# Two-layer hybrid encoder: the loaded up-projection weights begin 64 bytes behind a multiple of 256

## Chip, cores and metric

The kernel runs on 1 core of one Trainium2 chip, in one launch. The metric is the device time of the whole program in microseconds (us), lower is better; the time before is the median of 3 runs. TensorE (PE) does the matmuls and has its own weight-load queue (PEld), VectorE (DVE) and ScalarE (ACT) do the elementwise work, GpSimd (POOL) a little of it, and SyncE (SP) issues the transfers.

## Reference, cut to what matters

Two layers over 256 tokens of width 2048, all in float32. Each layer is a mixer (windowed attention beside a bidirectional mLSTM) between two large projections, and an MLP with a squared ReLU:

```
h   = rms_norm(x, g_pre_mix)
mix = concat(attention, mlstm)(h @ w_in) @ w_out      # w_in 2048x4624, w_out 2048x2048
x   = x + rms_norm(mix, g_post_mix)
h   = rms_norm(x, g_pre_mlp)
u   = square(relu(h @ w_up))                          # w_up 2048x8192
x   = x + rms_norm(u @ w_down, g_post_mlp)            # w_down 8192x2048
```

## The kernel before

**Three products for one.** Each float32 matrix is split into two parts of type float32r, `hi` (a rounded copy) and `lo` (the rest). A product is made of three matmuls: hi times hi, hi times lo, lo times hi. For weights, `load` does the split: SyncE fetches a piece of 1 MB into `raw` (2 buffers), ACT copies it to `whi` (line 188), DVE subtracts to get `wlo` (line 189). `whi` and `wlo` have 4 buffers each in pool `wsp`. Tokens are split in the same way and stand transposed in tiles of pool `tpool` (`hT`, `attT`, `memT`, `h2T`, `uT`), 16 KB per partition, the two parts of a block of 128 features side by side.

**Two forms of a stage.** A stage is a matrix block of 2048 x 512 (four pieces). In the streaming form (`mm_tile`, `mm_k`, lines 200 to 202) TensorE loads a 128 x 128 block of the tokens and streams 512 columns of the weights past it; the result has tokens on the partitions. All of w_in, w_out, w_down and the first up stage of each layer are done so. In the stationary form (`mm_stationary`, lines 269 to 271) it loads a 128 x 128 block of the weights and streams all 256 tokens past it, so that the result comes out transposed, as the down projection wants it. The other 15 up stages of each layer are done so: 15 stages x 64 blocks x 3 = 2880 matmuls a layer, 5760 in all. `stationary(key)` says which form a stage has. Each matmul, in both forms, has a weight load of its own.

**Addresses.** A partition's tiles follow each other in the order of the pools. The small tiles of pool `edge` come first and end at byte 2048. In the program before, every T tile, every `whi`, `wlo` and `raw` buffer begins at a multiple of 256 bytes, and within a stationary piece the blocks are 512 bytes apart, within a T tile 512 or 1024. One input stage (number 3: the gates with a part of q and k) is 272 columns wide, so that its blocks, 1088 bytes apart, begin 0, 64, 128 and 192 bytes behind a multiple of 256 in turn.

**Order.** The stages run in the order of `STAGES`. `mm_tile` and `mm_stationary` call `load` for their own stage and the one after, and `pump` puts steps of the mixer's side work between the matmuls of the input stages. The side work's temporaries of 1 KB (`rbt`, `cy`, `cth`, `kw`, `qw`, `ht`) share pool `f1k`.

Of the kernel before, what the change touches and what calls it, by code (L numbers as in the profile page):

```python
# [11 lines left out]
F32R = mybir.dt.float32r  # L12
# [5 lines left out]
P = 128  # L18
# [57 lines left out]
def stationary(key):  # L76


    _, st, b, n = key
    return st == "up" and (b, n) != (0, 0)  # L80
# [6 lines left out]
def encoder_kernel(ctx, tc, x, wall, rope, conv_w, gate_bias, ml_g, sink, gpre, gpost, out):  # L87
# [3 lines left out]
    wsp = ctx.enter_context(tc.tile_pool(name="wsp", bufs=4))  # L91
# [2 lines left out]
    apool = ctx.enter_context(tc.tile_pool(name="apool", bufs=1))  # L94
    gpool = ctx.enter_context(tc.tile_pool(name="gpool", bufs=3))
    f2k = ctx.enter_context(tc.tile_pool(name="f2k", bufs=8))
    f1k = ctx.enter_context(tc.tile_pool(name="f1k", bufs=5))
    small = ctx.enter_context(tc.tile_pool(name="small", bufs=3))
    lay = ctx.enter_context(tc.tile_pool(name="lay", bufs=2))
    psmm = ctx.enter_context(tc.tile_pool(name="psmm", bufs=2, space=bass.MemoryType.PSUM))  # L100
# [57 lines left out]
    order = []  # L158
# [9 lines left out]
    def load(i, begin=None):  # L168


        if i >= len(order) or order[i] in pieces:
            return
        o, w = offs[order[i]]
        k, n = (KC, P) if stationary(order[i]) else (PK, w)
        got = []
        for q in range(NPC):
            raw = wraw.tile([P, k, n], F32, tag="raw", name="raw")
            a = o + q * P * k * n
            src = wall[a:a + P * k * n].rearrange("(p k n) -> p k n", p=P, k=k)
            if begin is not None:  # L180
                begin(q)
            hi = wsp.tile([P, k, n], F32R, tag="hi", name="whi")
            lo = wsp.tile([P, k, n], F32R, tag="lo", name="wlo")
            step = 1 if begin is not None and q < 2 else k
            for j in range(0, k, step):
                sl = slice(j, j + step)
                nc.sync.dma_start(raw[:, sl], src[:, sl])
                nc.scalar.activation(hi[:, sl], raw[:, sl], AF.Copy)  # L188
                nc.vector.tensor_tensor(out=lo[:, sl], in0=raw[:, sl], in1=hi[:, sl].bitcast(F32), op=ALU.subtract)  # L189
            got.append((hi, lo))  # L190
        pieces[order[i]] = got
# [25 lines left out]
    def mm_tile(key, T, stages=(), after=None, at=None, half=False):  # L217

        load(pos[key])
        load(pos[key] + 1)
        if stages:
            ps = [psmm.tile([P, NT, 512], F32, tag="mm", name="mm")[:, 0] for _ in range(NT)]
# [30 lines left out]
    def mm_stationary(key, T, after):  # L256

        load(pos[key])  # L260
        load(pos[key] + 1)
        both = psmm.tile([P, 2, 512], F32, tag="mm", name="mms")
        for pair in range(2):
            ps = both[:, pair].rearrange("p (i t) -> p i t", i=2)
            for i in range(2):
                hi, lo = pieces[key][2 * pair + i]
                for k in range(KC):
                    Tk = T[k // 8][:, k % 8]
                    nc.tensor.matmul(ps[:, i], lhsT=hi[:, k], rhs=Tk[:, 0], start=(k == 0), stop=False)  # L269
                    nc.tensor.matmul(ps[:, i], lhsT=hi[:, k], rhs=Tk[:, 1], start=False, stop=False)  # L270
                    nc.tensor.matmul(ps[:, i], lhsT=lo[:, k], rhs=Tk[:, 0], start=False, stop=(k == KC - 1))  # L271
            after(pair, ps)
# [369 lines left out]
    def begin(q):  # L642
        if q:
            load_x(1, q - 1)
            load_x(0, q)
# [310 lines left out]
```

## Time and profile before

| | us |
|---|---|
| median of 3 runs | 2176.94 |
| the runs | 2176.94, 7516.22, 2171.56 |
| the profiled execution | 2173.81 |
| its span, first to last instruction | 2172.0 |
| PE busy, PEld busy | 2130.1, 1884.1 |
| DVE busy, ACT busy | 1136.4, 983.3 |

The profiled execution lies 0.14% under the median; 1.8 us of it lie outside the span. The records of matmuls overlap (a record of a 256-column float32r matmul lasts 0.28 us while one starts every 0.12 us), so a matmul's price is the distance from its start to the next one's start, and not its record's length.

### The profile page before, as it was taken

The numbers are of one execution on the slowest core, as the hardware profiler recorded it, in microseconds if no ns is written. First come the engines' busy times: TensorE is split into PE (matmuls) and PEld (weight loads), VectorE is DVE, ScalarE is ACT, GpSimd is POOL, SyncE is SP. The second block draws the span as 40 slices with busy tenths as digits, with TensorE's granted clock in tenths as the row PEclk, the third lists the DMA queues.
The fourth block names the chain that finished last, engine by engine and source line by source line (L and its number), as shares of the span: only waits on it lengthen the run. The fifth ranks groups of instructions, "written<-read, shape, count | busy, mean of one in ns | idle before, by whom it ended". The sixth has DMA issues, their size and how long they took to land.

```text
span 2172.0 us, 28977 instructions
## 1 busy us (share of the span) xinstructions
PE 2130.1 (98%) x12412; PEld 1884.1 (87%) x12412; DVE 1136.4 (52%) x1219; ACT 983.3 (45%) x1077; POOL 60.7 (3%) x68
## 2 busy tenths in 40 slices
PE   8999999999999999999999999999999999999998
PEld 6878887988998998898878788879889989989986
DVE  6666566444445444445576656464444444444454
ACT  6445445443443443344354555354444434433542
POOL 0000003000000000000020000030000000000000
PEclk9999999999999999999999999999999999999999
DMA  7534354555545555546544344545554555554553
GB/s 254 175 133 162 136 202 146 194 197 194 190 177 194 177 189 196 193 157 210 175 177 168 126 146 156 201 157 178 210 194 176 187 192 181 179 194 174 185 207 116
DMA packets 62209, 388.37 MB, mean 179 GB/s; under 512 B 9600, under 2 KB 10112, under 8 KB 17280
## 3 DMA queue, kind: packets, MB, share of 16 engines
q1 hardware_dynamic: 61936, 386.48, 50.8%
q8 instruction: 97, 1.59, 0.3%
q14 instruction: 32, 0.26, 0.0%
q10 hardware_dynamic: 144, 0.03, 0.0%
HBM read 384.39 MB, written 2.10 MB: 178 GB/s over the span
## 4 chain that ended last, share of the span: by engine, by line
PE 93%; DVE 2%; ACT 2%; DMA 1%; POOL 1%; issue 1%; SPq 0%; POOLq 0%; DVEq 0%; ACTq 0%
PE mm L202 19%; PE mm L201 19%; PE mm L200 19%; PE mms L269 11%; PE mms L271 11%; PE mms L270 11%; DMA raw<-wall 1%; PE pn L591 1%; PE sc L375 1%; DVE xs L789 1%; PE po L414 1%; DVE wlo L189 1%; POOL h2T L322 0%; ACT uz L845 0%; ACT whi L188 0%
## 5 line engine op out<-in xcount | busy, mean ns | idle before, releaser
L189 DVE TENSOR_TENSOR wlo<-raw,whi 128x2048 fp32r<-128x2048 f32 (+3 forms) x374 | 828.7, 2217 | 907.2 <-ACT whi L188 906.7
L188 ACT ACTIVATE whi<-raw 128x2048 fp32r<-128x2048 f32 (+3 forms) x374 | 692.9, 1853 | 943.9 <-PE mm L202 514.6
L269 PE MATMUL mms<-h2T,whi 128*128 128x256 f32 x1920 | 544.4, 284 | 7.3 <-ACT uz L845 7.3
L270 PE MATMUL mms<-h2T,whi 128*128 128x256 f32 x1920 | 542.6, 283 | 0.0
L271 PE MATMUL mms<-h2T,wlo 128*128 128x256 f32 x1920 | 539.8, 283 | 0.0
L201 PE MATMUL mm<-wlo,uT 128*128 128x512 f32 x1024 | 398.4, 389 | 0.0
L200 PE MATMUL mm<-whi,uT 128*128 128x512 f32 x1024 | 398.4, 389 | 0.0
L202 PE MATMUL mm<-whi,uT 128*128 128x512 f32 x1024 | 398.1, 389 | 0.0
L269 PEld LDWEIGHTS mms<-h2T,whi 128*128 128x128 f32 x1920 | 368.4, 192 | 11.9 <-ACT uz L845 11.5
L270 PEld LDWEIGHTS mms<-h2T,whi 128*128 128x128 f32 x1920 | 368.4, 192 | 0.3
L271 PEld LDWEIGHTS mms<-h2T,wlo 128*128 128x128 f32 x1920 | 366.9, 192 | 0.0
L200 PE MATMUL mm<-whi,hT 128*128 128x512 f32 (+2 forms) x640 | 242.6, 380 | 8.7 <-ACT hT L321 6.5
L202 PE MATMUL mm<-whi,hT 128*128 128x512 f32 (+2 forms) x640 | 242.0, 379 | 0.3 <-POOL hT L322 0.2
L201 PE MATMUL mm<-wlo,hT 128*128 128x512 f32 (+2 forms) x640 | 241.3, 377 | 0.2 <-DVE wlo L189 0.2
L201 PEld LDWEIGHTS mm<-wlo,uT 128*128 128x128 f32 x1024 | 192.2, 188 | 40.0
L200 PEld LDWEIGHTS mm<-whi,uT 128*128 128x128 f32 x1024 | 192.2, 188 | 39.5
L202 PEld LDWEIGHTS mm<-whi,uT 128*128 128x128 f32 x1024 | 192.2, 188 | 39.4
L200 PEld LDWEIGHTS mm<-whi,hT 128*128 128x128 f32 x640 | 121.9, 190 | 29.1 <-ACT hT L321 7.4
L202 PEld LDWEIGHTS mm<-whi,hT 128*128 128x128 f32 x640 | 121.7, 190 | 21.9 <-POOL hT L322 1.2
L201 PEld LDWEIGHTS mm<-wlo,hT 128*128 128x128 f32 x640 | 121.9, 191 | 20.4 <-DVE wlo L189 0.5
L866 DVE SCALAR_TENSOR_TENSOR A_mlp<-mm,s2q,A_mlp 128x512 f32<-128x512 f32 x48 | 34.0, 747 | 37.0 <-PE mm L202 37.0
L200 PE MATMUL mm<-whi,memT 128*128 128x512 f32 x128 | 50.4, 394 | 0.0
(221 smaller groups left out, 1463.8 us busy)
## 6 DMA issues: line engine op xcount, KB each, us to landing
raw<-wall SPq DMA_DIRECT2D x350, 1024.0 KB, 4.8
raw<-wall SPq DMA_DIRECT2D x8, 544.0 KB, 3.6
g<-gpost SPq DMA_DIRECT2D x16, 256.0 KB, 4.5
raw<-wall SPq DMA_DIRECT2D x8, 512.0 KB, 3.3
xs<-x_in SPq DMA_DIRECT2D x8, 256.0 KB, 5.2
raw<-wall SPq DMA_DIRECT2D x8, 256.0 KB, 6.6
y_out<-xs SPq DMA_DIRECT2D x8, 256.0 KB, 2.8
cossin<-rope SPq DMA_DIRECT2D x1, 256.0 KB, 7.0
```

The lines of the kernel that those rows point to most:

```text
L188: nc.scalar.activation(hi[:, sl], raw[:, sl], AF.Copy)
L189: nc.vector.tensor_tensor(out=lo[:, sl], in0=raw[:, sl], in1=hi[:, sl].bitcast(F32), op=ALU.subtract)
L200: nc.tensor.matmul(dst, lhsT=xh, rhs=hi, start=(k == 0), stop=False)
L201: nc.tensor.matmul(dst, lhsT=xh, rhs=lo, start=False, stop=False)
L202: nc.tensor.matmul(dst, lhsT=xl, rhs=hi, start=False, stop=(k == KC - 1))
L269: nc.tensor.matmul(ps[:, i], lhsT=hi[:, k], rhs=Tk[:, 0], start=(k == 0), stop=False)
L270: nc.tensor.matmul(ps[:, i], lhsT=hi[:, k], rhs=Tk[:, 1], start=False, stop=False)
L271: nc.tensor.matmul(ps[:, i], lhsT=lo[:, k], rhs=Tk[:, 0], start=False, stop=(k == KC - 1))
L375: nc.tensor.matmul(sc[:, j], lhsT=qT[:, q0 + j, t * P:(t + 1) * P], rhs=kT[:, g], start=(j == 0), stop=False)
L414: nc.tensor.matmul(po[:, j], lhsT=vA[:, kb, g * HD:(g + 1) * HD], rhs=pT[:, kb], start=(kb == 0), stop=(kb == 1))
L591: nc.tensor.matmul(pn[:, :DV + 1], lhsT=dt[:, d, c], rhs=va[:, c, h], start=True, stop=(c == c1))
L866: nc.vector.scalar_tensor_tensor(out=acc[:, t, sl], in0=ps, scalar=s2[t], in1=acc[:, t, sl], op0=ALU.mult, op1=ALU.add)
```

## The change

The `whi` and `wlo` buffers get 64 elements (256 bytes) more. A stage of the stationary form uses its buffer from element 16 on, which is 64 bytes behind the buffer's start; a stage of the streaming form uses it from element 0. A buffer is 2112 x 4 = 8448 bytes, 33 times 256, so all buffers still begin at a multiple of 256. Eight buffers take 2048 bytes more; pool `f1k` gives up one of its five buffers (1024 bytes). No instruction is added or removed, and all shapes stay.

```diff
-    f1k = ctx.enter_context(tc.tile_pool(name="f1k", bufs=5))
+    f1k = ctx.enter_context(tc.tile_pool(name="f1k", bufs=4))
...
-            hi = wsp.tile([P, k, n], F32R, tag="hi", name="whi")
-            lo = wsp.tile([P, k, n], F32R, tag="lo", name="wlo")
+
+            o1 = 16 if stationary(order[i]) else 0
+            hi, lo = (
+                wsp.tile([P, 2048 + 64], F32R, tag=x, name=f"w{x}")[:, o1:o1 + k * n].rearrange(
+                    "p (k n) -> p k n", k=k) for x in ("hi", "lo"))
```

## Rows read from the trace of the kernel before

**Rows 1.** The page's busy time by engine, and TensorE's granted clock in 40 slices.
```profile
PE 2130.1 (98%) x12412; PEld 1884.1 (87%) x12412; DVE 1136.4 (52%) x1219; ACT 983.3 (45%) x1077; POOL 60.7 (3%) x68
...
PEclk9999999999999999999999999999999999999999
```
**Rows 2.** The page's chain that ended last, by engine and by line.
```profile
PE 93%; DVE 2%; ACT 2%; DMA 1%; POOL 1%; issue 1%; SPq 0%; POOLq 0%; DVEq 0%; ACTq 0%
PE mm L202 19%; PE mm L201 19%; PE mm L200 19%; PE mms L269 11%; PE mms L271 11%; PE mms L270 11%; DMA raw<-wall 1%; PE pn L591 1%; PE sc L375 1%; DVE xs L789 1%; PE po L414 1%; DVE wlo L189 1%; POOL h2T L322 0%; ACT uz L845 0%; ACT whi L188 0%
```
**Rows 3.** Windows (PE, PEld, DVE, ACT, POOL, clock, DMA, GB/s): stationary, then streaming.
```profile
600.00:620.00 20.00, 20.00 (x169) 20.00 (x168) 6.32 (x4) 8.61 (x8) 0.00 (x0) 1.00 0.44 159
700.00:720.00 20.00, 20.00 (x90) 16.55 (x89) 8.84 (x6) 7.67 (x4) 0.00 (x0) 1.00 0.58 200
```
**Rows 4.** Waits, 390 to 1080 us: total us, times, longest us.
```profile
ACT whi L188 <- PE mms L270: 159.1, 40, 7.0
ACT whi L188 <- DMA raw<-wall: 16.2, 18, 4.5
```
**Rows 5.** Groups by line: count, busy us, mean ns, idle before and its end.
```profile
L269 PE MATMUL mms<-h2T,whi 128*128 128x256 f32 x1920 | 544.4, 284 | 7.3 <-ACT uz L845 7.3
```
**Rows 6.** Timeline of TensorE in a stationary stage: first and last of 16 matmuls (start, duration).
```profile
596.68 0.28 PE L271 MATMUL mms<-h2T,wlo 128*128 128x256 f32 x1
...
598.48 0.28 PE L271 MATMUL mms<-h2T,wlo 128*128 128x256 f32 x1
```
**Rows 7.** Timeline of TensorE in a down stage: first and last of 18 matmuls.
```profile
699.62 0.39 PE L200 MATMUL mm<-whi,uT 128*128 128x512 f32 x1
...
703.47 0.39 PE L202 MATMUL mm<-whi,uT 128*128 128x512 f32 x1
```
**Rows 8.** Timeline: plain float32 matmuls (four in a row), then streams behind them.
```profile
74.99 1.02 PE L375 MATMUL sc<-scr 128*128 128x256 f32 x4
...
75.97 0.40 PE L202 MATMUL mm<-whi,hT 128*128 128x512 f32 x1
76.20 0.40 PE L200 MATMUL mm<-whi,hT 128*128 128x512 f32 x1
76.44 0.39 PE L201 MATMUL mm<-wlo,hT 128*128 128x512 f32 x1
...
77.13 0.39 PE L201 MATMUL mm<-wlo,hT 128*128 128x512 f32 x1
```
**Rows 9.** Line 375 alone: duration in ns, least, median and most.
```profile
L375 PE MATMUL sc<-scr x64: 377/379/635, 75.0 to 1212.7; 128*128 128x256 f32 x64
```
**Rows 10.** Timeline of the 272-column stage: first of each six matmuls, four blocks.
```profile
98.36 0.28 PE L200 MATMUL mm<-whi,hT 128*128 128x272 f32 x1
...
99.11 0.28 PE L200 MATMUL mm<-whi,hT 128*128 128x272 f32 x1
...
99.86 0.29 PE L200 MATMUL mm<-whi,hT 128*128 128x272 f32 x1
...
100.62 0.28 PE L200 MATMUL mm<-whi,hT 128*128 128x272 f32 x1
...
101.36 0.39 PE L200 MATMUL mm<-whi,hT 128*128 128x512 f32 x1
```
**Rows 11.** Weight loads by line: stationary stages, then down stages.
```profile
L270 PEld LDWEIGHTS mms<-h2T,whi 128*128 128x128 f32 x1920 | 368.4, 192 | 0.3
...
L200 PEld LDWEIGHTS mm<-whi,uT 128*128 128x128 f32 x1024 | 192.2, 188 | 39.5
```
**Rows 12.** Timeline of VectorE around the fullest moment of pool `f1k`.
```profile
64.42 0.87 DVE L357 SCALAR_TENSOR_TENSOR rbt<-mm,r_s,cossin 128x256 f32<-128x256 f32 x2
...
65.86 0.86 DVE L357 SCALAR_TENSOR_TENSOR rbt<-mm,r_s,cossin 128x256 f32<-128x256 f32 x2
66.64 0.75 DVE L360 TENSOR_TENSOR ra<-ra,rbt 128x256 f32<-128x256 f32 x2
...
69.51 0.75 DVE L360 TENSOR_TENSOR ra<-ra,rbt 128x256 f32<-128x256 f32 x2
```

## Prediction

> **What bounds the kernel now.** I read the page's busy times first, then the chain, then windows by stage, then single starts on the timeline. TensorE is busy 98% of the span at the granted clock of the upper level (2.4 GHz) in every slice [rows 1], and 93% of the chain is TensorE's own work: 57% in the streaming lines 200 to 202, 32% in the stationary lines 269 to 271 [rows 2]. In a stationary stretch and in a streaming one there is no idle time on it at all, while VectorE and ScalarE work less than half of the time [rows 3]. The weights are no bound there: the split's first step waits for TensorE to give its buffers back, 159.1 us in 40 waits on the stationary line alone, and for the transfer only 16.2 us in 18 [rows 4]. TensorE waits for the stationary results' evacuation 7.3 us in all [rows 5]. So the time is the number of matmuls times the distance of their starts, and the change can act on that distance alone.
>
> **What a matmul costs.** Sixteen stationary matmuls start at 596.68 to 598.48 us: 1.80 us over 15 steps, 120.0 ns each [rows 6]. The 256 columns take 256/2.4 = 106.7 ns, so 13.3 ns are extra. In the down stage 17 steps take 3.85 us, 226.5 ns each for 512 columns (213.3 ns): the same 13 ns [rows 7]. The extra belongs to the matmul, or to its load, and not to the columns. Plain float32 matmuls have nearly none of it: four of them last 1.02 us from first start to last end [rows 8], each lasts 379 ns [rows 9], so the starts are (1020 - 379)/3 = 214 ns apart, for 256 columns at half rate (213.3 ns); the printed hundredths leave this open by some 3 ns, and I take 2 ns of extra. They too have a load each. What costs 11 ns arises, then, where a load and a stream at full rate read together. All of them begin at multiples of 256 bytes now. That is what the change alters, for 3 x 1920 = 5760 matmuls [rows 5]; 1 ns on each is 5.76 us, 0.26% of the time.
>
> **The change part by part.** *The 64 bytes.* No row of before shows a load that begins 64 bytes behind its stream. Bound from below: the 2 ns of the plain float32 rows instead of 13.3 ns, 11 ns x 5760 = 63 us less [rows 8, 9]. Bound from above: behind a disturbance, with the same addresses, streams start up to 0.24 us apart (76.20 to 76.44) and five steps take 1.16 us, 232 ns each, before they settle to 226.7 [rows 8]; the largest is some 9 ns over the settled distance, and 9 x 5760 = 52 us more. That the distance moves at all with equal addresses says that the extra is no fixed price but hangs on how load and stream fall together in time.
> The nearest row is the 272-column stage. There the loaded tokens begin at a multiple of 256 and the streamed weights 0, 64, 128 and 192 bytes behind one, block after block. The six matmuls of a block take 0.75, 0.75, 0.76 and 0.74 us [rows 10], which is 125.0, 125.0, 126.7 and 123.3 ns each, for 272/2.4 = 113.3 ns of columns: an extra of 11.7, 11.7, 13.3 and 10.0 ns. The fourth is the one in which the load stands 64 bytes past the stream modulo 256, as after the change. If a shift by 64 bytes freed the readers of each other, one of the four would have shown 115 ns. None did. The difference between the fourth and the first is 1.7 ns, printed to within 3 ns, and between the fourth and the settled 13.3 ns it is 3.3 ns. I take 1.5 ns less, 1.5 x 5760 = 8.6 us, with 3 ns less and 2 ns more as its own bounds (-17 to +12 us). Against that row speaks that its offset lasts six matmuls only, in which a pattern that needs several to settle (rows 8) may not have come about; so both far ends stay open.
> The Trainium skill speaks against any effect: "SBUF — State Buffer", section "Who interferes with whom", gives TensorE two independent read ports, one for the streamed operand and one for the load, and says that it never waits on anyone. By that the sum would be nothing for this part; the 13 ns that float32r streams pay and plain float32 ones don't, and the unsettled 232 ns, fit it badly.
> *A shorter stationary stage.* At the lower bound a stage of 192 matmuls takes 20.9 us in place of 23.0, still not under the 96 x 226.5 ns = 21.7 us of a streaming one by much, whose weights come in time at 200 GB/s [rows 3]. The waits of the split are for TensorE, so a gain in it would not be taken back by the transfers.
> *The load's own length* is recorded as 192 ns in the stationary stages and 188 in the down stages [rows 11]; a change of these 4 ns goes along with the distance and is not counted again.
> *One temporary less in `f1k`.* The fullest moment that I find has four buffers in use: two pairs of `rbt` are written at 64.42 and 65.86 us and read at 66.64 and 69.51 us [rows 12]. The fullest moment elsewhere is no fuller, worked out from first write and last read of each user. So four suffice and the sum has +1 us for it; should VectorE wait at the four such places as long as its step between the two reads (2.9 us less 0.75 us), it is 9 us. Its cover is that TensorE has the input stages' matmuls to go on with.
> *Copies and subtractions* into a buffer that begins 64 bytes on: same shapes, and both engines have room [rows 3]; nothing.
>
> **The sum.** The profiled execution took 2173.8 us, its span 2172.0 and 1.8 outside; the median of the runs is 3.1 us above it, and I start between them, at 2175. 2175 - 9 + 1 = 2167 us.
>
> **The rivals.** *The address is of no account* (what costs is the load itself, at any address). For it: the four offsets of rows 10 give nearly the same. Then 2175 + 1 = 2176 us.
> *Load and stream stop colliding.* For it: the plain float32 rows show that a load need not cost more than 2 ns, and the extra is equal in both forms. Against it: rows 10. Between 109 and 112 ns in place of 120: 46 to 63 us less, 2112 to 2129 us. The Trainium skill's "TensorE: Matmul & The Clock Gate", section "Back-to-back issue gap", has N/2.4 + 2.5 ns for a warm matmul alone, which is 109.2 ns here; the trace's 120 is over it, and the gap between them is 62 us, about this rival's most.
> *The shifted load falls into a worse pattern and stays there*, the other side: what rows 8 show for some matmuls becomes the settled state of the stationary stages. Unsettled steps average 232 against 226.7, 5 ns; 4.5 ns x 5760 = 26 us, 2201 us. It is slower as soon as the distance settles above 120 ns, and by over 2% (43.5 us) from 127.6 ns on, near the largest single step seen.
> *Only the lost temporary is felt*: 2175 + 9 = 2184 us.
>
> **How the numbers follow.** Forecast (a small gain, 2159 to 2188 as its own range) 0.38; no account 0.22; no collision 0.24; worse pattern 0.11; temporary 0.05. The likeliest is 2167 us. The range must take in the collision rival, with which, the address rival and the temporary it holds 0.89: from 2112, less 2 for the runs' scatter, to 2190, 2110 to 2190 us. About 2% is what a measurement of this kernel can tell from no change. Faster by over 2% (under 2133 us) is the collision rival but for a part of it, 0.22; slower by over 2% (above 2220 us) is the end of the worse pattern, 0.05; within 2%, 0.73.
>
> **What would show it.** Starts on the timeline of a stationary stage after the change: 117 to 122 ns apart is the forecast or the address rival (exactly 120.0 is the latter), 109 to 112 the collision rival, 124 and more the worse pattern. The down stages should stay at 226.5 ns, TensorE's share of the busy time and the clock should stay, and ScalarE's wait for line 270 should be there still; if a gain on the distance doesn't reach the time, its idle time before line 269 will have grown. The temporary's cost would show as VectorE's waits before `rbt` and `cth` and as TensorE's idle time before 280 us and between 1105 and 1360 us. I am wrong if the settled distance in the stationary stages isn't what the short runs of rows 10 let expect: a pattern that settles over hundreds of equal matmuls can end elsewhere.

## The result, and the profile after

The changed kernel took 2144.73 us (median of 4 runs, 2141.79 to 2146.77) against 2174.25 us before (median of 4 runs: 2168.82, 2171.56, 2176.94 and 7516.22). The run of 7516.22 us counts in that median, as in the 2176.94 us of the prediction; without it the median before is 2171.56 us. The ratio leaves it out: 0.987, 95% interval 0.984 to 0.990. The profiled execution has a span of 2143.4 us, 28.6 us under that of before. All lines behind the diff have moved by three: 200 to 202 are 203 to 205, 269 to 271 are 272 to 274.

The page of the changed kernel, busy time by engine, then the chain by engine and by line; it answers to [rows 1, 2]:

```profile
PE 2100.0 (98%) x12412; PEld 1855.3 (87%) x12412; DVE 1135.4 (53%) x1219; ACT 983.9 (46%) x1077; POOL 60.8 (3%) x68
...
PE 92%; DVE 2%; DMA 2%; ACT 2%; POOL 1%; issue 1%; SPq 1%; POOLq 0%; DVEq 0%; ACTq 0%
PE mm L205 19%; PE mm L204 19%; PE mm L203 19%; PE mms L272 10%; PE mms L274 10%; PE mms L273 10%; DMA raw<-wall 1%; PE sc L378 1%; PE pn L594 1%; DVE xs L792 1%; PE po L417 1%; DVE wlo L192 1%; POOL h2T L325 1%; ACT whi L191 0%; ACT uz L848 0%
```

The reader is to see that counts and DVE and ACT stay, that TensorE's busy time falls by 30.1 us, about what the span lost, and that of TensorE's lines in the chain the stationary ones alone lose a share. TensorE is as much the bound as before.

The groups by line of the changed kernel, which answer to [rows 5, 11]:

```profile
L272 PE MATMUL mms<-h2T,whi 128*128 128x256 f32 x1920 | 535.2, 279 | 7.0 <-ACT uz L848 6.8
...
L273 PEld LDWEIGHTS mms<-h2T,whi 128*128 128x128 f32 x1920 | 362.3, 189 | 0.3
```

The waits of the changed kernel from 390 to 1080 us, which answer to [rows 4]:

```profile
ACT whi L191 <- PE mms L273: 126.6, 33, 6.8
ACT whi L191 <- DMA raw<-wall: 35.7, 25, 3.6
```

TensorE's idle time before a stationary line is 7.0 us (7.3 before). The recorded load is 3 ns shorter, and that of the down stages stays at 188. The split still waits for TensorE first of all; its wait for transfers is up from 16.2 us, but TensorE didn't wait for it, so the weights are no bound.

The timeline of TensorE in the changed kernel, which answers to [rows 6, 7]: first and last of 21 matmuls of a stationary stage, a wait in it, first and last of 22 matmuls behind that wait, and first and last of 17 matmuls of a down stage:

```profile
559.81 0.28 PE L274 MATMUL mms<-h2T,wlo 128*128 128x256 f32 x1
...
562.16 0.28 PE L273 MATMUL mms<-h2T,whi 128*128 128x256 f32 x1
...
573.47 0.28 PE L272 MATMUL mms<-h2T,whi 128*128 128x256 f32 x1
573.59 0.28 PE L273 MATMUL mms<-h2T,whi 128*128 128x256 f32 x1
574.32 0.39 PE L272 MATMUL mms<-h2T,whi 128*128 128x256 f32 x1 [0.45 <-ACT uz L848]
574.54 0.28 PE L273 MATMUL mms<-h2T,whi 128*128 128x256 f32 x1
574.66 0.28 PE L274 MATMUL mms<-h2T,wlo 128*128 128x256 f32 x1
...
575.25 0.28 PE L273 MATMUL mms<-h2T,whi 128*128 128x256 f32 x1
575.36 0.28 PE L274 MATMUL mms<-h2T,wlo 128*128 128x256 f32 x1
...
589.75 0.28 PE L274 MATMUL mms<-h2T,wlo 128*128 128x256 f32 x1
...
592.13 0.28 PE L274 MATMUL mms<-h2T,wlo 128*128 128x256 f32 x1
...
699.66 0.39 PE L204 MATMUL mm<-wlo,uT 128*128 128x512 f32 x1
...
703.28 0.39 PE L205 MATMUL mm<-whi,uT 128*128 128x512 f32 x1
```

2.35/20 is 117.5 ns, 2.38/21 is 113.3 ns, 3.62/16 is 226 ns. There are two distances where there was one: group by group of 48 matmuls (one weight buffer) the stationary stages start 117.8 ns or 113.3 ns apart, in nearly all groups from first to last (120.0 before), and the streaming stages haven't moved. Between the two places lies the wait at 573 us. TensorE stands still there for 0.45 us, until ScalarE has taken the results out; some seven matmuls follow at 0.12 us, and then it goes on at 0.11 (113.3) for stages. Instructions and addresses modulo 256 are the same on both sides of that wait. The buffers themselves, 33 times 256 bytes apart, begin at even and odd multiples of 256 in turn, and the groups from all of them start alike: no period longer than 256 bytes shows.

From the starts on the timeline I sum two times for each kernel. S is the time of all stretches of stationary matmuls, each from its first start to the next streaming matmul's start; T is the rest of the span from the first streaming start on. Before: S 698.4, T 1465.0 us. After: S 670.8, T 1464.2 us. So 27.6 of the span's 28.6 us were won in the stationary stages, 27.6/5760 = 4.8 ns on each matmul.

### The profile page after: what moved, and what is told of

Its sections match the earlier page's. It is cut to its first block, busy times and chain, and to the rows that moved or that the text cites. A ratio compares the mean times of both kernels' runs of the same rounds, so it can differ in the third digit from the quotient of the medians.

```text
span 2143.4 us, 28980 instructions
## 1 busy us (share of the span) xinstructions
PE 2100.0 (98%) x12412; PEld 1855.3 (87%) x12412; DVE 1135.4 (53%) x1219; ACT 983.9 (46%) x1077; POOL 60.8 (3%) x68
## 4 chain that ended last, share of the span: by engine, by line
PE 92%; DVE 2%; DMA 2%; ACT 2%; POOL 1%; issue 1%; SPq 1%; POOLq 0%; DVEq 0%; ACTq 0%
PE mm L205 19%; PE mm L204 19%; PE mm L203 19%; PE mms L272 10%; PE mms L274 10%; PE mms L273 10%; DMA raw<-wall 1%; PE sc L378 1%; PE pn L594 1%; DVE xs L792 1%; PE po L417 1%; DVE wlo L192 1%; POOL h2T L325 1%; ACT whi L191 0%; ACT uz L848 0%
## 5 line engine op out<-in xcount | busy, mean ns | idle before, releaser
L272 PE MATMUL mms<-h2T,whi 128*128 128x256 f32 x1920 | 535.2, 279 | 7.0 <-ACT uz L848 6.8
L273 PE MATMUL mms<-h2T,whi 128*128 128x256 f32 x1920 | 533.3, 278 | 0.0
L274 PE MATMUL mms<-h2T,wlo 128*128 128x256 f32 x1920 | 530.5, 278 | 0.0
L272 PEld LDWEIGHTS mms<-h2T,whi 128*128 128x128 f32 x1920 | 360.7, 188 | 11.8 <-ACT uz L848 11.1
L273 PEld LDWEIGHTS mms<-h2T,whi 128*128 128x128 f32 x1920 | 362.3, 189 | 0.3
L274 PEld LDWEIGHTS mms<-h2T,wlo 128*128 128x128 f32 x1920 | 360.0, 188 | 0.0
```

## The experiments

Three theories stood. *Distance*: what counts is how far the loaded block stands from the streamed one, modulo some multiple of 64 bytes. *Own start*: a load that begins at 64 modulo 256 is cheaper by itself. *By-product*: the moved buffers or the smaller `f1k` pool change the order or the waits. All edits below are to the changed kernel; the distance is load minus stream, modulo 256 bytes.

| kernel | stationary distance | streaming distance | time, us | S, us | T, us | stationary starts, ns | 512-column starts, ns |
|---|---|---|---|---|---|---|---|
| before | 0 | 0 | 2174.25 | 698.4 | 1465.0 | 120.0 | 226.7 |
| changed | 64 | 0 | 2144.73 | 670.8 | 1464.2 | 113.3 or 117.8 | 226.7 |
| e1 | 0 | 0 | 2175.21 | 698.5 | 1466.7 | 120.0 | 226.7 |
| e4 (all moved) | 0 | 0 | 2172.66 | 698.5 | 1464.2 | 120.0 | 226.7 |
| e7 | 32 | 0 | 2166.05 | 689.1 | 1466.6 | 118.3 | 226.7 |
| e8 | 96 | 0 | 2156.58 | 684.0 | 1462.7 | 117.3 or 118.6 | 226.7 |
| e2 | 128 | 0 | 2169.51 | 693.6 | 1465.9 | 118.6 or 120.0 | 226.7 |
| e3 | 192 | 0 | 2155.05 | 680.5 | 1465.1 | 113.3 or 117.8 | 226.7 |
| e6 | 64 | 192 | 2149.64 | 664.9 | 1477.5 | 113.3 or 117.8 | 229 |
| e5 | 64 | 64 | 2170.01 | 663.6 | 1496.0 | 113.3 or 117.8 | 233.3 |
| e10 | 64 | 128 | 2175.51 | 674.6 | 1491.0 | 113.3 or 117.8 | 232.4 |
| e9 | 64 | 0, last piece 64 | 2142.09 | 665.4 | 1464.9 | 113.3 or 117.8 | 226.7 |
| e11 | 64 | 0, 272 columns 64 | 2148.31 | 674.2 | 1464.0 | 113.3 or 117.8 | 226.7 |
| e12 | 64 | 0 | 2146.97 | 671.9 | 1465.9 | 113.3 or 117.8 | 226.7 |

The times of e5, e6, e9 and e12 are medians of several runs, those of e1 to e4, e7, e8, e10 and e11 single ones; the runs of the kernel before beside them have medians of 2171 to 2173 us. The starts are medians of the settled groups (for 512 columns in e5, e6 and e10 the mean, since they settle less).

**e1, the room alone.**

```diff
-            o1 = 16 if stationary(order[i]) else 0
+            o1 = 0 if stationary(order[i]) else 0
```

> The wider buffers and the f1k pool of four, but every stage from element 0 on. If the 64 bytes are the cause of the 30 us, stationary starts are 120.0 ns apart again and the time is that of before, 2168 to 2177 us. If the moved buffers or the smaller pool (through another order on the engines) are the cause, starts stay between 113 and 118 ns apart and the time near 2145 us.

2175.21 us beside 2172.82 before. First and last of 22 stationary matmuls of e1 on the timeline:

```profile
599.83 0.28 PE L273 MATMUL mms<-h2T,whi 128*128 128x256 f32 x1
...
602.35 0.28 PE L273 MATMUL mms<-h2T,whi 128*128 128x256 f32 x1
```

2.52/21 = 120.0 ns. The by-product theory falls: S is that of before to 0.1 us, T 1.7 us more, which is within what T differs by between runs (1463 to 1467 us in kernels that share it).

**e4, everything moved by 64 bytes.**

```diff
-    nhalf = edge.tile([P, 16], F32, name="nhalf")
+    nhalf = edge.tile([P, 32], F32, name="nhalf")
...
-            o1 = 16 if stationary(order[i]) else 0
+            o1 = 0 if stationary(order[i]) else 0
```

> A small tile ahead of the pools grows by 64 bytes, so tokens, streamed and loaded weights all begin 64 bytes behind a multiple of 256; no stage has an offset of its own. Relative-offset theory: the distance is nothing again, 120 ns in the stationary and 226.7 in the streaming stages, about 2172 us. Own-start theory (a load that begins at 64 modulo 256 is cheaper by itself): stationary 113 to 118 ns, about 2145 us, and the streaming stages, whose loaded tokens then begin at 64 too, nearer 222 ns, about 2115 us in all.

2172.66 us. First and last of 22 stationary matmuls, then of 17 in a down stage of e4:

```profile
599.77 0.28 PE L273 MATMUL mms<-h2T,whi 128*128 128x256 f32 x1
...
602.29 0.28 PE L273 MATMUL mms<-h2T,whi 128*128 128x256 f32 x1
...
699.65 0.39 PE L205 MATMUL mm<-whi,uT 128*128 128x512 f32 x1
...
703.27 0.39 PE L203 MATMUL mm<-whi,uT 128*128 128x512 f32 x1
```

120.0 and 226 ns: a load that begins at 64 modulo 256 wins nothing when its stream does too. The own-start theory falls, and the distance stands.

**e2, e3, e7, e8, other distances.** Each is one number.

```diff
-            o1 = 16 if stationary(order[i]) else 0
+            o1 = 32 if stationary(order[i]) else 0
```

This is e2: 32 elements are 128 bytes. e3 has 48 in its place, e7 8 and e8 24.

> Stationary stages begin 128 bytes behind a multiple of 256. Relative-offset theory (what counts is how far the load stands from the stream, in 64-byte steps modulo 256): two steps apart is at least as good as one, 113 to 118 ns and 2130 to 2150 us. Theory of only one good place (the load must run just one step ahead): back to 120 ns and 2170 us.

> Stationary stages begin 192 bytes behind, that is 64 before a multiple of 256. Relative-offset theory: the load now runs one step behind the stream instead of ahead; if any distance frees them, 113 to 118 ns (2130 to 2150 us); if the order matters, 120 ns or more (2170 to 2200 us). The 272-column rows of before had this as their second block, 125.0 ns against 123.3 in the fourth, which would give a smaller gain than with 64, 2155 to 2165 us.

> Stationary stages begin 32 bytes behind. If the readers collide in units of 64 bytes, half a unit still leaves them together for half the time: 117 to 120 ns, 2155 to 2172 us. If the unit is 16 or 32 bytes, 113 to 118 ns as with 64, near 2145 us.

> Stationary stages begin 96 bytes behind, between 64 (113 and 118 ns) and 128 (118.6 and 120 ns). If the pattern repeats every 128 bytes, this lies between the two or equals the case of 32 bytes mirrored, 117 to 119 ns, 2155 to 2168 us; if any odd distance frees the readers, 113 to 118 ns and 2130 to 2145 us.

Timelines of the stationary stages, one fence for each kernel. e2, at two places (23 matmuls each, 120.0 and 118.6 ns):

```profile
555.74 0.28 PE L273 MATMUL mms<-h2T,whi 128*128 128x256 f32 x1
...
558.38 0.28 PE L274 MATMUL mms<-h2T,wlo 128*128 128x256 f32 x1
...
599.77 0.28 PE L273 MATMUL mms<-h2T,whi 128*128 128x256 f32 x1
...
602.38 0.28 PE L274 MATMUL mms<-h2T,wlo 128*128 128x256 f32 x1
```

e3 (24 matmuls, 113.5 ns; then 23 matmuls, 117.7 ns):

```profile
409.73 0.28 PE L273 MATMUL mms<-h2T,whi 128*128 128x256 f32 x1
...
412.34 0.28 PE L272 MATMUL mms<-h2T,whi 128*128 128x256 f32 x1
...
589.76 0.28 PE L273 MATMUL mms<-h2T,whi 128*128 128x256 f32 x1
...
592.35 0.28 PE L274 MATMUL mms<-h2T,wlo 128*128 128x256 f32 x1
```

e8 (23 matmuls, 117.3 ns):

```profile
599.81 0.28 PE L274 MATMUL mms<-h2T,wlo 128*128 128x256 f32 x1
...
602.39 0.28 PE L273 MATMUL mms<-h2T,whi 128*128 128x256 f32 x1
```

Two steps of 64 bytes are not as good as one: 128 wins 4.8 us of S, 64 and 192 win 27.6 and 17.9. 64 and 192 share their two distances between starts to the tenth; they differ in how many groups are in which. The wait of 0.45 us shown above comes once in each of the six runs of stationary stages behind a down projection; at 64 bytes it takes the starts from 117.8 to 113.3 ns in five of the six in the first profile and in all six in e12, at 192 in none. 32 and 96 lie between (9.3 and 14.4 us), as the expectation for 64-byte units had it. The expectation that any two steps do as well was wrong; a period near 128 bytes fits these six points, but 0 and 128 aren't equal.

**e5, e6, e10, the streaming stages too.**

```diff
-            o1 = 16 if stationary(order[i]) else 0
+            o1 = 16 if stationary(order[i]) else 48
```

This is e5: 48 elements are 192 bytes. e6 has 16 in its place and e10 32.

> The changed kernel, and the streaming stages' weights begin 192 bytes behind a multiple of 256, so that there too the loaded block (tokens, at a multiple of 256) stands 64 bytes past the streamed one modulo 256. If the distance is what counts in both forms, 512-column starts fall from 226.7 ns to between 220 and 224.5 ns (16 to 27 cycles of 2.4 GHz over the columns, as the stationary ones did), 13 to 40 us under the changed kernel: 2105 to 2132 us. If the gain is one of 256-column streams alone (load and stream there are nearly as long as each other), starts stay at 226.7 ns and the time at 2145 us.

> The same with the streaming stages' weights at 64 bytes: the loaded tokens then stand 192 past the streamed weights. With 192 the stationary stages gained less often but reached the same two distances; so 220 to 224.5 ns for 512 columns and 2105 to 2135 us if the distance is what counts in both forms, 2145 us if it is a matter of the stationary form alone.

> The changed kernel, and streams at 128 bytes in all streaming stages. For 512 columns 64 and 192 gave about 229 and 233 ns against 226.7 at 0. If a pattern of 128 bytes repeats there too, 226 to 228 ns and 2140 to 2150 us; if 0 is the one good place for long streams, 229 to 234 ns and 2155 to 2180 us.

First and last of 17 matmuls of a down stage of e5:

```profile
699.72 0.39 PE L205 MATMUL mm<-whi,uT 128*128 128x512 f32 x1
...
703.46 0.39 PE L203 MATMUL mm<-whi,uT 128*128 128x512 f32 x1
```

3.74/16 = 234 ns, against 226 with no distance. Neither expectation held: it is no gain and no standstill, but a loss. For 512 columns each distance tried is worse than 0: 229 (192), 232.4 (128), 233.3 ns (64); T grows by 13.4, 26.8 and 31.9 us over the changed kernel's. e5 ends at 2170.01 us (ratio 0.999, 0.997 to 1.000), e6 at 2149.64 (0.989, 0.986 to 0.992). It is the columns, not the form: the one streaming stage of 256 columns in each layer starts 114.8 ns apart in e5, on the mean of its settled starts, against 119.6 in the changed kernel. And S falls to 663.6 in e5: its stationary stages behind the down projection now settle at 113.3 from the start.

**e9, the last piece.** From that follows a version that could beat both: only the matmuls right before a stationary stage, and the 256-column input stage, get the other distance.

```diff
             o1 = 16 if stationary(order[i]) else 0
+            if not stationary(order[i]) and (w == 256 or q == NPC - 1 and i + 1 < len(order) and stationary(order[i + 1])):
+                o1 = 48
```

> The changed kernel, and in a streaming stage that stands right before a stationary one the last of four pieces begins at 192 bytes (as do all pieces of the 256-column input stage). If which of its two distances (113.3 or 117.8 ns) a stationary stage settles in is handed on by the pattern of the matmuls before it, the stages behind the down projection settle at 113.3 as they did with all streams at 192: about 2500 matmuls by 4.4 ns, 11 us, less some 2 us for slower streams: 2132 to 2138 us. If the state is drawn by the offset of the whole streaming part or by chance, 2143 to 2147 us.

> The changed kernel once more, beside the three others on their chip: 2141 to 2147 us, 1.1% to 1.5% under the kernel before, with the same stages at 117.8 and at 113.3 ns as in its first profile if the state is handed on by what stands before, other stages if it is chance.

First and last of 22 matmuls of e9 (113.3 ns), where the changed kernel, run again as e12, has 21 matmuls at 118 ns:

```profile
556.80 0.28 PE L275 MATMUL mms<-h2T,whi 128*128 128x256 f32 x1
...
559.18 0.28 PE L275 MATMUL mms<-h2T,whi 128*128 128x256 f32 x1
```

```profile
559.75 0.28 PE L274 MATMUL mms<-h2T,wlo 128*128 128x256 f32 x1
...
562.11 0.28 PE L273 MATMUL mms<-h2T,whi 128*128 128x256 f32 x1
```

Behind the down projection six runs of stationary stages begin. In the first profile of the changed kernel, in e11, in e12 and in e10 (streams at a distance of 128) all six begin at 117.8 ns; in e9, and in e5 and e6 before it, all six begin at 113.3. So the state at the start is handed on by the pattern before it.

Later it may change at a wait for ScalarE. The program has eight runs of stationary stages, the six and two behind the first up stages. Before the last 96 matmuls of each TensorE waits once more, with one streaming matmul ahead of the wait, and there two profiles of the same program differ. First and last of the matmuls behind one such wait, in the first profile of the changed kernel (11 from 618.82 on, 114 ns) and in e12 (14 from 618.41 on, 118 ns):

```profile
618.60 0.39 PE L272 MATMUL mms<-h2T,whi 128*128 128x256 f32 x1 [0.45 <-ACT uz L848]
618.82 0.28 PE L273 MATMUL mms<-h2T,whi 128*128 128x256 f32 x1
...
619.96 0.28 PE L274 MATMUL mms<-h2T,wlo 128*128 128x256 f32 x1
```

```profile
618.18 0.39 PE L272 MATMUL mms<-h2T,whi 128*128 128x256 f32 x1 [0.45 <-ACT uz L848]
618.41 0.28 PE L273 MATMUL mms<-h2T,whi 128*128 128x256 f32 x1
...
619.94 0.28 PE L274 MATMUL mms<-h2T,wlo 128*128 128x256 f32 x1
```

Over the whole program it is 113.3 behind eight of eight such waits in the first profile and behind one of eight in e12. What decides there is open; within a profile it looks too regular for plain chance.

S of e9 is 6.5 us under e12's; the time is 2142.09 (ratio 0.986, 0.983 to 0.988) against 2146.97 us (0.988, 0.987 to 0.990). The intervals overlap: the trace shows the gain, the times don't separate it. The expected 2132 to 2138 us was not reached: later in e9 a wait takes some groups back to 117.8.

**e11, the 272-column stage made even.**

```diff
-            o1 = 16 if stationary(order[i]) else 0
+            o1 = 16 if stationary(order[i]) else 48 if n == 272 else 0
+            pitch = 320 if n == 272 else n
             hi, lo = (
-                wsp.tile([P, 2048 + 64], F32R, tag=x, name=f"w{x}")[:, o1:o1 + k * n].rearrange(
-                    "p (k n) -> p k n", k=k) for x in ("hi", "lo"))
+                wsp.tile([P, 2048 + 64], F32R, tag=x, name=f"w{x}")[:, o1:o1 + k * pitch].rearrange(
+                    "p (k n) -> p k n", k=k)[:, :, :n] for x in ("hi", "lo"))
```

> The changed kernel, and in the 272-column input stage the blocks stand 1280 bytes apart (a multiple of 256) from byte 192 on, so that the load stands 64 bytes past the stream in every block and not in one of four. If the rows of before misled because their offset lasts only six matmuls, starts fall from 125 ns on the mean to between 118 and 122 ns (113.3 and 5 to 9 more). If 272 columns don't settle at all, since they are no multiple of 32, 123 to 127 ns as before. The time hardly moves either way (192 matmuls): 2141 to 2147 us.

First and last of 45 matmuls of that stage in e11:

```profile
96.02 0.29 PE L204 MATMUL mm<-whi,hT 128*128 128x272 f32 x1
...
101.45 0.29 PE L206 MATMUL mm<-whi,hT 128*128 128x272 f32 x1
```

5.43/44 = 123.4 ns, against 125 on the mean before [rows 10]: in the range of the second expectation (123 to 127, as before) at its lower end, and within the rows' reading what the fourth block showed (123.3). At the distance of 64 bytes 272 columns cost some 10 ns over their 113.3, whether it lasts six matmuls or the stage. The undisturbed starts of this stage keep to that one distance in both layers.

## Why the prediction was right in its direction and its range, and short in its size

- *What bounds the kernel* held. Only the distance of the starts moved, TensorE's waits before the stationary lines hardly did, and the weights came in time (the split's wait for transfers grew from 16.2 to 35.7 us without reaching TensorE).
- *The 64 bytes* is the term that was mis-sized: 1.5 ns was taken, -8.6 us, with 3 ns as its furthest gain; the trace shows 4.8 ns, 27.6 us. The forecast's own range, 2159 to 2188, missed 2144.73 for this in the main; some 3 us more lie in its start at 2175, pulled up by the run of 7516.22 us. That the whole range held is owed to the collision rival, which had been taken in, and not to the forecast. Of the signs it named, 117 to 122 ns fits the slower distance, and 113.3 lies in none of its windows.
- The step behind it that failed is "the nearest row": the 272-column rows were carried over to 256 columns. They were read rightly, and their short runs didn't falsify them (e11). At 64 bytes 272 columns pay some 10 ns over their columns, and the slower of the two distances of 256 columns pays 11.1, near to it; but the faster one, at which over half of the stationary matmuls run, pays 6.7, and no row had it. "One of the four would have shown 115 ns" was no test for 256 columns. That a distance's worth hangs on the stream's length is shown for 512 columns, which pay 20.0 ns at 64 bytes, while 256 and 512 alike pay 13.3 at 0; for 272 against 256 it isn't, since no run shows whether 272 columns have a faster distance too. The prediction's last sentence, that a pattern over hundreds of equal matmuls can end elsewhere, named what came.
- *The collision rival* had the right sign and too large a size: 109 to 112 ns were forecast, 113.3 was reached in part of the groups and 117.8 in the rest. That load and stream collide in the memory is its reading of this; the runs show that their addresses count, and not what happens between them.
- *The address is of no account* is refuted: e1 and the changed kernel differ in nothing but the addresses of the stationary stages' weights (120.0 against 113.3 or 117.8 ns), and e4 shows that it is the distance from the stream that counts. This case doesn't agree with what the Trainium skill says under "SBUF — State Buffer", section "Who interferes with whom", that TensorE's two read ports are independent and that it never waits on anyone: how its own two reads lie to each other moved its starts by 2.2 to 6.7 ns.
- *The worse pattern* didn't come in the stationary stages, but it exists: e5 and e10 show it for 512 columns, 6.6 and 5.7 ns more, and there it cancels the gain. (Its price was worked out with 4.5 ns, 26 us, where the rows' 5 ns give 29 us; nothing else rests on it.)
- *The lost temporary* at +1 us agrees with e1 (S equal, T 1.7 us more), which can't be told from nothing.
- *The load's own length* went along with the distance, 192 to 188 or 189 ns.

Open: why the pattern has two settled distances, what chooses between them behind a wait, and why 64 bytes help most. The runs show their effect, not the memory's layout.

## What to carry to other kernels

When every float32r matmul has a load of its own and the starts stand further apart than the columns ask for, the addresses of the two operands are worth a sweep: shift the loaded one against the streamed one in steps of 64 bytes, once for each stream length. Keep the distance that is best for each length, here 64 bytes for 256 columns and 0 for 512, and don't carry one length's row to another. Read the starts on the timeline in groups: a mean over two settled states hides both.

## What was unexpected of the hardware

The same instructions at the same addresses settle at 113.3 or at 117.8 ns and stay there for hundreds of matmuls; what ran before the stage decides at its start (six of six at 113.3 in e9 against none of six in e12), and a wait of 0.45 us can switch it. And the distance that helps 256-column streams by 2.2 to 6.7 ns harms 512-column ones by 6.6.
